# A smaller ring of DMA descriptors and two more slots for expert weights

## The chip, the cores and the metric

The kernel runs on one core of a Trainium2 chip. The core has TensorE (PE, matmuls), VectorE (DVE), ScalarE (ACT), GpSimd (POOL) and SyncE (SP); here SyncE issues nearly all DMAs. The metric is the device time of one execution in microseconds; lower is better.

## The reference

One layer of an encoder block on 256 tokens of width 1024, in float32. A normed input goes through one wide projection; its columns feed sparse attention (16 heads) and a Mamba-2 scan (SSD, 32 heads in 4 groups). Both branches are gated, merged and projected, and the sum goes through a mixture of experts, which is where most bytes are read: all weights of 32 experts, 1024 x 256 for gate and up and 256 x 1024 for down.

```python
h = rmsnorm(x, attn_norm);  proj = h @ w_in
...
x = x + (sigmoid(gate_a) * (y_attn @ w_attn) + sigmoid(gate_b) * (y_ssd @ w_ssd)) @ w_out
hf = rmsnorm(x, ffn_norm)
...
for g in range(4):
    a = einsum('nd,edf->nef', hf, w_gate[g])
    u = einsum('nd,edf->nef', hf, w_up[g])
    act = silu(a) * u * combine[:, g, :, None]
    out = out + einsum('nef,efd->nd', act, w_down[g])
x = x + out
```

`combine` is zero but for two experts of a token.

## The kernel before, in words

**Dense part (to some 385 us).** The weights of the projections come as chunks `w0` to `w37`. Class `Chunk` (line 130) issues their loads on SyncE (`w_raw`, line 141); `split_hi` on ScalarE (line 152) and `split_lo` on VectorE or GpSimd (line 156) cut each into two float32r parts, `w_hl`, which TensorE uses in three passes (lines 241, 294). A `w_raw` load waits until the buffer that it overwrites has been split; four such buffers are cycled.

**Order of the work.** The program is written as Python loops, and a scheduler that simulates a time line sets the order in which each engine issues its instructions. The loop at line 808 takes the SSD groups 1 to 3: for each of four chunks it multiplies, then calls `prefetch(PF0[4 * g + i])`, then one step of the scan of the group before. `PF0` (line 1199) has a string for each of these 12 places and for 4 behind them; a letter is one chunk of expert weights that is loaded there, and names the pool of buffers that it goes to.

**Expert part.** The experts' weights are 96 chunks of 128 partitions x 4 experts x 512 numbers (8 KB of a partition, 1.05 MB): eight quarters `q` (0 to 7) of four experts, each with eight chunks for gate and up (`wgu`, k = 0 to 7) and four for down (`wdn`). `prefetch` (line 255) loads the next chunk on SyncE:

```python
n = len(ewt)
q, i = divmod(n, 12)
src = wgu[q, i] if i < KD else wdn[q, i - KD]
etags.append(tag)
m = 2 if tag in "RSG" else 4
for e in range(0, 4, m):
    w = bigt([P, m, 512], F32, f"we{q}_{i}", tag)
    for cols in (slice(0, 256), slice(256, 512)) if n == 95 else (slice(0, 512),):
        nc.sync.dma_start(w[:, :, cols], src[:, e:e + m, cols])
```

Letters R, S and G take a chunk in two pieces of two experts, so with two loads; the other letters take it whole. The last chunk, 95, is loaded in two halves of its columns besides. The letters of the dense part are the slots of a ring: `ring = list(etags)` (line 1013), and chunk n takes the slot of chunk n less the number of slots, once TensorE has used that one (line 1016). Before the change the ring has 23 slots: five E, two H, two A, four of `PF1`, three of `PFO`, and two R, three S and two G at line 914.

A quarter is: gather of its tokens by matmul (line 1030), gate and up (line 1037), the activation on ScalarE and VectorE (lines 1073 to 1076), transposes (line 1079), down (line 1097), and the sum over experts into `acc` (line 1112). In the last quarter `warm2` (line 862) puts matmuls without use between these steps. The output is copied and stored from line 1114 on. A fallback for overfull experts (line 1124) is not taken.

`kernel` (line 1297) builds the program. The memory that is kept for GpSimd's ring of DMA descriptors has its default size, 16 KB of a partition.

Of the kernel before, what the change touches and what calls it, by code (L numbers as in the profile page):

```python
# [48 lines left out]
def block_kernel(ctx, tc, xin, idn, ngain, catt, cprep, cssd, cmoe, cwr, wsm, wwide, win, wgu, wdn, out, dbg=None):  # L49
# [205 lines left out]
    def prefetch(tags):  # L255

        for tag in tags:
            n = len(ewt)
            if n == 96:
                return  # L260
# [4 lines that stand above are left out]
            v = []  # L265
            with tc.issue_after(last_raw[0].ins):
# [4 lines that stand above are left out]
                    v += [w[:, j, :] for j in range(m)]  # L271
            ewt.append(v)
# [513 lines left out]
    def steps(g, names):  # L786

        for n in names:
            with tc.high_priority(HP["XEYT".index(n.upper())]):
                if n in "Xx":  # L790
                    ssd_x(g, "Xx".index(n))
                elif n in "Ee":
                    ssd_e(g, "Ee".index(n))
                elif n in "Yy":
                    ssd_y(g, "Yy".index(n))
                elif g:
                    ssd_tail(g - 1)
# [10 lines left out]
    for g in range(3):  # L808
        for i, c in enumerate(group_chunks(g + 1)):
            c()  # L810
            prefetch(PF0[4 * g + i])
            steps(g, SEQ[i])
    for c in range(2):
        def half(i):
            prefetch(PF0[12 + i])
            steps(3, SEQ[i])
# [379 lines left out]
XD = 2  # L1196
YB = 2
SEQ = ("XE", "xYTe", "y", "")
PF0 = ('EEEEE',) + 10 * ('',) + ('HH', '', '', '', 'AA')
NE = "".join(PF0).count("E")  # L1200
XB = 3
ZB = 2
# [107 lines left out]
```

## Time and profile before

| | us |
|---|---|
| median of 3 runs | 589.68 (589.41 to 589.89) |
| profiled execution | 591.09 |
| its span, first to last instruction | 589.3 |
| TensorE busy | 558.2 (95%) |
| VectorE, ScalarE, GpSimd busy | 331.0, 272.1, 241.8 |
| bytes moved | 159.27 MB, mean 270 GB/s |

The profile is of one execution whose own time is 1.4 us above the median; 1.8 us of it lie outside the span. Busy time of TensorE is modelled at its ends and includes waits of the pipeline, so a share of 95% isn't a share of its peak. The profile's share of a DMA engine counts the time of its packets, so a mean share of 1.01 means that all 16 are always busy. "Landing" is the time from the issue of a load to its arrival.

### The profile page before, as it was taken

How to read it: one execution, taken by the hardware profiler on the slowest of the kernel's cores; microseconds unless marked ns; L12 is line 12 of the kernel's file. 1: busy time of each engine (PE TensorE's matmuls, PEld its weight loads, DVE VectorE, ACT ScalarE, POOL GpSimd, SP SyncE). 2: the span in 40 equal slices, each digit the busy share in tenths (PEclk: the TensorE clock that was granted, in tenths of full speed). 3: DMA queues.
4: the chain of work that ended last, by engine and by line, in shares of the span. 5: the costliest groups of instructions: out<-in, count | busy, mean ns of one | idle time of the engine just before them, and what ended most of it. 6: DMA issues, size and time to landing. Idle time of an engine off the chain costs nothing.

```text
span 589.3 us, 9910 instructions
## 1 busy us (share of the span) xinstructions
PE 558.2 (95%) x3605; PEld 401.8 (68%) x3605; DVE 331.0 (56%) x689; ACT 272.1 (46%) x633; POOL 241.8 (41%) x254
## 2 busy tenths in 40 slices
PE   8999989999999999999999999999898898896996
PEld 5878768798898999888878888954353354241422
DVE  4669974999995888999595656441111211110101
ACT  7567567658897688877763535500000000000001
POOL 5677685666764376575767644210000000000000
PEclk9999999999999999999999999999999998987899
DMA  6755244353434585445767599999999999999994
GB/s 269 253 176 180 71 160 162 118 182 132 131 122 161 177 365 208 143 137 162 252 220 254 176 329 409 400 340 414 418 413 414 418 419 409 417 419 420 409 412 140
DMA packets 35811, 159.27 MB, mean 270 GB/s; under 512 B 4144, under 2 KB 5808, under 8 KB 27184
## 3 DMA queue, kind: packets, MB, share of 16 engines
q1 hardware_dynamic: 34464, 157.30, 70.8%
q10 hardware_dynamic: 1296, 1.30, 0.6%
q8 instruction: 30, 0.49, 0.3%
q14 instruction: 21, 0.17, 0.1%
HBM read 157.54 MB, written 1.05 MB: 269 GB/s over the span
## 4 chain that ended last, share of the span: by engine, by line
PE 71%; DMA 14%; DVE 7%; issue 3%; POOL 3%; ACT 2%; SPq 0%; ACTq 0%; DVEq 0%; POOLq 0%
DMA we<-wgu 8%; PE ps_xs L241 8%; PE ps_S L294 7%; PE pgu L1037 6%; PE ps_z L241 6%; PE ps_g L294 6%; DMA we<-wdn 5%; PE py L1097 4%; PE ps_g L1030 4%; PE ps_A L294 4%; PE acc L1112 3%; PE ps_q L294 2%; PE ps_o L241 2%; PE ps_o L294 2%; PE ps_iq L294 2%
## 5 line engine op out<-in xcount | busy, mean ns | idle before, releaser
L156 POOL TENSOR_TENSOR w_hl<-w_raw,w_hl 128x512 fp32r<-128x512 f32 (+1 forms) x101 | 140.9, 1399 | 88.2 <-ACT w_hl L152 67.2
L152 ACT CAST w_hl<-w_raw 128x512 fp32r<-128x512 f32 (+1 forms) x212 | 125.7, 619 | 49.1 <-PE ps_S L294 19.0
L156 DVE TENSOR_TENSOR w_hl<-w_raw,w_hl 128x512 fp32r<-128x512 f32 (+1 forms) x111 | 98.5, 895 | 37.3 <-ACT w_hl L152 36.6
L1037 PE MATMUL pgu<-we,xg 128*32 128x512 f32 x512 | 63.1, 603 | 4.0 <-DMA we<-wgu 4.0
L1055 POOL TENSOR_TENSOR dc<-Dm,cmr 128x128 f32<-128x128 f32 x16 | 6.1, 401 | 141.2 <-DVE Dm L960 135.1
L241 PE MATMUL ps_z<-hT,w_hl 128*128 128x256 f32 x384 | 51.5, 286 | 0.0
L241 PE MATMUL ps_xs<-hT,w_hl 128*128 128x256 f32 x384 | 50.7, 285 | 0.0
L241 PEld LDWEIGHTS ps_z<-hT,w_hl 128*128 128x128 f32 x384 | 47.7, 190 | 2.0 <-issue 1.8
L241 PEld LDWEIGHTS ps_xs<-hT,w_hl 128*128 128x128 f32 x384 | 47.5, 191 | 2.1 <-issue 2.1
L294 PE MATMUL ps_g<-w_hl,gT 128*128 128x512 f32 x192 | 47.9, 398 | 0.0
L294 PE MATMUL ps_S<-w_hl,yT 128*128 128x512 f32 x192 | 44.9, 392 | 0.0
L1033 DVE TENSOR_TENSOR xg<-ps_g,cmoe 128x512 f32<-128x512 f32 (+2 forms) x18 | 11.3, 631 | 57.2 <-PE ps_g L1030 57.1
L1030 PEld LDWEIGHTS ps_g<-Dm,x_sb 128*128 128x128 f32 x256 | 31.3, 191 | 17.0 <-issue 13.5
L1037 PEld LDWEIGHTS pgu<-we,xg 128*32 128x32 f32 x512 | 15.3, 110 | 40.0 <-issue 25.9
L1097 PE MATMUL py<-we,aTt 128*32 128x512 f32 (+1 forms) x272 | 37.7, 683 | 3.9 <-DVE aTt L1083 2.1
L294 PEld LDWEIGHTS ps_g<-w_hl,gT 128*128 128x128 f32 x192 | 35.1, 188 | 8.8 <-issue 0.8
L294 PEld LDWEIGHTS ps_S<-w_hl,yT 128*128 128x128 f32 x192 | 35.7, 188 | 7.6 <-issue 0.2
L1075 DVE SCALAR_TENSOR_TENSOR ac<-th,pgu 128x256 f32<-128x256 f32 x8 | 3.4, 421 | 59.9 <-ACT th L1073 59.9
L1108 ACT COPY y<-py 128x512 f32<-128x512 f32 (+1 forms) x9 | 4.8, 538 | 67.2 <-PE py L1097 67.2
L1030 PE MATMUL ps_g<-Dm,x_sb 128*128 128x128 f32 x256 | 33.8, 280 | 0.0
L1112 PE MATMUL acc<-y,dcT 128*128 128x512 f32 (+1 forms) x68 | 32.4, 604 | 0.9 <-DVE y L1110 0.8
L1073 ACT ACTIVATE th<-pgu,rs 128x256 f32<-128x256 f32 x8 | 3.8, 473 | 59.6 <-PE pgu L1037 59.6
(296 smaller groups left out, 976.2 us busy)
## 6 DMA issues: line engine op xcount, KB each, us to landing
we<-wgu SPq DMA_DIRECT2D x42, 1024.0 KB, 14.3
w_raw<-wwide SPq DMA_DIRECT2D x60, 512.0 KB, 3.7
we<-wdn SPq DMA_DIRECT2D x25, 1024.0 KB, 13.9
w_raw<-win SPq DMA_DIRECT2D x44, 512.0 KB, 3.7
we<-wgu SPq DMA_DIRECT2D x44, 512.0 KB, 10.3
we<-wdn SPq DMA_DIRECT2D x14, 512.0 KB, 10.2
x_sb<-xin SPq DMA_DIRECT2D x2, 512.0 KB, 4.3
w_raw<-wsm SPq DMA_DIRECT2D x1, 512.0 KB, 5.5
```

The costliest lines, as they stand in the source:

```text
L152: return act.copy(self.hl[i][:, 0], self.raw[i])
L156: return eng.tensor_sub(hl[:, 1], self.raw[i], hl[:, 0].bitcast(F32))
L241: pe.matmul(ps, lhsT=lhs[k][:, a], rhs=rhs[k][:, b], start=j == 0 and k == 0 and i == 0, stop=j == len(regions) - 1 and k == KD - 1 and i ...
L294: pe.matmul(ps[t], lhsT=lhs[t][k][:, a], rhs=w[k][:, b], start=k == 0 and i == 0, stop=k == KD - 1 and i == 2)
L1030: pe.matmul(ps[:, kk, :], lhsT=x1[:, t, (k + kk) * P:(k + kk + 1) * P], rhs=Dm[:, t].rearrange("p e j -> p (e j)"), start=t == 0, stop=t == 1)
L1033: dve.tensor_tensor(xg[:, ks, :], ps, fgain[:, ks].unsqueeze(2).to_broadcast([P, n, P]), op=ALU.mult)
L1037: i = pe.matmul(pgu[32 * e:32 * e + 32, :], lhsT=xg[:, k, 32 * e:32 * e + 32], rhs=wg[k][e], start=k == 0, stop=k == KD - 1, tile_position ...
L1055: pool.tensor_tensor(dc[:, t], Dm[:, t], cmr[:, t, 4 * q:4 * q + 4].unsqueeze(2).to_broadcast([P, 4, NSLOT]), op=ALU.mult)
L1073: act.activation(th, pgu[:, 0:256], AF.Tanh, scale=rs)
L1097: i_py = pe.matmul(py[32 * e:32 * e + 32, :], lhsT=aTt[:, f, 32 * e:32 * e + 32], rhs=wd[2 * n + f][e][:, c], start=f == 0, stop=f == 1, t ...
L1108: act.copy(y, py)
L1112: pe.matmul(acc[t][n][:, c], lhsT=dcT[:, t * P:(t + 1) * P], rhs=y, start=False, stop=q == 7 and c.stop == 512)
```

## The change

The memory kept for GpSimd's descriptors is set to 512 bytes of a partition. `PF0` has two more letters E, at the places 5 and 7 (group 2's second and fourth chunk of the loop), so `NE`, the number of buffers of pool E, becomes 7, and the ring 25 slots. The chunks that are loaded at the later places are each two further on, and the slots R, S and G now hold other chunks.

```diff
-PF0 = ('EEEEE',) + 10 * ('',) + ('HH', '', '', '', 'AA')
+PF0 = ('EEEEE',) + 4 * ('',) + ('E', '', 'E', '', '', '', 'HH', '', '', '', 'AA')
 NE = "".join(PF0).count("E")
...
-    nc = _bacc.Bacc("TRN2", target_bir_lowering=False, num_devices=1)
+
+    nc = _bacc.Bacc("TRN2", target_bir_lowering=False, num_devices=1, dynamic_dma_scratch_size=512)
```

First, SyncE's queue in the dense part, behind the first five chunks (`we_4` is chunk 4 of a quarter, `w_raw` the weights for the split); the difference:

```order
 L270 DMA we_3_2497<-wgu 128x2048
 L270 DMA we_4_2499<-wgu 128x2048
-L141 DMA w_raw<-win 128x1024 x12
+L141 DMA w_raw<-win 128x1024 x2
+L270 DMA we_5_3004<-wgu 128x2048
+L141 DMA w_raw<-win 128x1024 x4
+L270 DMA we_6_3228<-wgu 128x2048
+L141 DMA w_raw<-win 128x1024 x6
 L141 DMA w_raw<-wwide 128x1024 x5
```

Chunks 5 and 6 are issued among the loads of `w23` to `w28`; where chunk 5 stood, behind `wwide`, there is now chunk 7.

Second, TensorE in the last quarter, the down matmuls of the second half of the columns (`we_10` is chunk 94, `we_11` chunk 95, `acc` the sum over experts, `py` the product for 32 slots of an expert). Before:

```order
L1097 MATMUL py<-we_10_5701,aTt 32x256 x4
L1112 MATMUL acc_4740<-y,dcT 128x512
L1112 MATMUL acc_4742<-y,dcT 128x512
L1097 MATMUL py<-we_10_5701,aTt 32x256 x4
L1097 MATMUL py<-we_11_5703,aTt 32x256 x8
L1112 MATMUL acc_4741<-y,dcT 128x256
```

Now:

```order
L1097 MATMUL py<-we_10_5689,aTt 32x256 x2
L1097 MATMUL py<-we_10_5691,aTt 32x256 x2
L1097 MATMUL py<-we_11_5693,aTt 32x256 x2
L1112 MATMUL acc_4744<-y,dcT 128x512
L1112 MATMUL acc_4746<-y,dcT 128x512
L1097 MATMUL py<-we_10_5689,aTt 32x256 x2
L1097 MATMUL py<-we_10_5691,aTt 32x256 x2
L1097 MATMUL py<-we_11_5693,aTt 32x256 x2
L1097 MATMUL py<-we_11_5696,aTt 32x256 x4
L1112 MATMUL acc_4745<-y,dcT 128x256
```

Both chunks now are in two pieces, and two matmuls on the first piece of chunk 95 stand ahead of the sums of the first half (`acc` 128x512), which stood right behind chunk 94.

Third, SyncE's last loads of quarter 7. Before:

```order
L270 DMA we_6_5689<-wgu 128x1024
L270 DMA we_6_5691<-wgu 128x1024
L270 DMA we_7_5693<-wgu 128x1024
L270 DMA we_7_5695<-wgu 128x1024
L270 DMA we_8_5697<-wdn 128x2048
L270 DMA we_9_5699<-wdn 128x2048
L270 DMA we_10_5701<-wdn 128x2048
L270 DMA we_11_5703<-wdn 128x4x256 x2
```

Now:

```order
L270 DMA we_6_5679<-wgu 128x2048
L270 DMA we_7_5681<-wgu 128x2048
L270 DMA we_8_5683<-wdn 128x2048
L270 DMA we_9_5685<-wdn 128x1024
L270 DMA we_9_5687<-wdn 128x1024
L270 DMA we_10_5689<-wdn 128x1024
L270 DMA we_10_5691<-wdn 128x1024
L270 DMA we_11_5693<-wdn 128x2x256 x2
L270 DMA we_11_5696<-wdn 128x2x256 x2
```

The chunks of gate and up came in halves and are now whole, and the last three down chunks were whole (95 by columns) and now come in pieces.

In the dense part the scheduler also orders TensorE, VectorE, ScalarE and GpSimd differently from the second half of group 1's steps on; the instructions are the same.

## Rows read from the trace of the kernel before

**Rows 1.** The page, busy share of the 16 DMA engines in 40 slices.
```profile
DMA  6755244353434585445767599999999999999994
```
**Rows 2.** Windows of all engines: start:end, length, busy (count), granted clock, DMA share, GB/s.
```profile
40.00:80.00 40.00, 38.23 (x187) 30.34 (x185) 35.50 (x68) 24.20 (x50) 28.87 (x31) 1.00 0.42 140
260.00:280.00 20.00, 20.00 (x153) 16.89 (x152) 20.00 (x40) 15.17 (x33) 11.89 (x10) 1.00 0.49 149
390.00:392.00 2.00, 2.00 (x20) 1.57 (x20) 0.00 (x0) 0.00 (x0) 0.00 (x0) 1.00 0.60 111
400.00:420.00 20.00, 19.44 (x136) 9.81 (x138) 3.81 (x9) 0.99 (x3) 0.76 (x2) 1.00 1.01 422
480.00:500.00 20.00, 17.89 (x131) 7.27 (x131) 3.41 (x9) 1.06 (x3) 0.76 (x2) 0.91 1.01 413
```
**Rows 3.** The chain in order of time, 370 to 590 us: start, length, what.
```profile
437.91 7.05 PE pgu L1037 x64
...
480.13 7.05 PE pgu L1037 x64
...
501.99 11.37 DMA we<-wdn
...
562.36 15.15 DMA we<-wdn
...
578.29 1.91 PE acc L1112 x4
```
**Rows 4.** Timeline of SyncE, 390 to 391 us: start, length, engine, line, operation.
```profile
390.15 0.33 SPq L270 DMA_DIRECT2D we<-wdn  x1
```
**Rows 5.** Line 270, issued 513.2 to 531.3 us (x8: min/median/max ns, first to last).
```profile
L270 SPq EVENT_SEMAPHORE  x8: 17/17/17, 513.4 to 530.8; - x8
...
DMA to landing us min/median/max: 19.9/19.9/19.9
```
**Rows 6.** Line 270, issued 550.6 to 559 us: halves of chunks.
```profile
L270 SPq DMA_DIRECT2D we<-wgu x7: 328/328/328, 550.8 to 558.5; - x7
...
DMA to landing us min/median/max: 10.1/10.2/10.2
```
**Rows 7.** Line 270, issued 563.5 to 566 us: the column halves of chunk 95.
```profile
L270 SPq DMA_DIRECT2D we<-wdn x2: 549/602/655, 563.6 to 564.9; - x2
...
DMA to landing us min/median/max: 15.3/15.4/15.5
```
**Rows 8.** The page, DMA queues: packets, MB, share of 16 engines' time.
```profile
q1 hardware_dynamic: 34464, 157.30, 70.8%
q10 hardware_dynamic: 1296, 1.30, 0.6%
```
**Rows 9.** Line 141, issued 210 to 215 us: loads for the split.
```profile
L141 SPq DMA_DIRECT2D w_raw<-win x2: 327/328/328, 210.8 to 213.6; - x2
...
DMA to landing us min/median/max: 11.9/12.0/12.1
```
**Rows 10.** The page, DMA issues: count, KB each, median us to landing.
```profile
w_raw<-win SPq DMA_DIRECT2D x44, 512.0 KB, 3.7
```
**Rows 11.** Waits of TensorE, 200 to 345 us: total, times, longest. The only row.
```profile
PE py L749 <- DVE e L734: 0.2, 1, 0.2
```
**Rows 12.** Windows of all engines, columns as in rows 2: quarters 6 and 7.
```profile
538.00:539.00 1.00, 0.68 (x4) 0.20 (x8) 0.00 (x0) 0.00 (x0) 0.00 (x0) 0.50 0.99 410
548.00:549.00 1.00, 1.00 (x10) 0.70 (x7) 0.00 (x0) 0.00 (x0) 0.00 (x0) 0.94 0.92 377
562.00:569.00 7.00, 5.89 (x30) 0.87 (x25) 0.00 (x0) 0.00 (x0) 0.00 (x0) 1.00 1.04 420
```
**Rows 13.** Timeline of TensorE, 535 to 570 us, with the idle time before a piece.
```profile
538.32 1.94 PE L1037 MATMUL pgu<-we,xg 128*32 128x512 f32 x8 [1.44 <-DMA we<-wgu]
543.13 5.24 PE L1097 MATMUL py<-we,aTt 128*32 128x512 f32 x24 [0.56 <-issue]
563.62 1.05 PE L1037 MATMUL pgu<-we,xg 128*32 128x512 f32 x4 [0.23 <-DMA we<-wgu]
```

## The prediction

> **What bounds the kernel now.** I read the 40 slices first, then the windows, then the chain in order of time, then the transfers behind the last waits.
>
> The slices show two regimes [rows 1]: in the first 23 of 40 the DMA engines are busy for 2 to 8 tenths, and from the 24th on they are full almost to the end. The windows give them numbers [rows 2]: at 260 to 280 us TensorE is busy for all of its 20.00 us while DMA moves 149 GB/s; at 400 to 500 us DMA has a share of 1.01 at 413 to 422 GB/s.
>
> The chain says what that costs [rows 3]. From 390 to 502 us it runs through TensorE, which has a store of loaded weights: the gate/up work of quarters 2 and 4 begins at 437.91 and 480.13 us, so a quarter takes TensorE 21.1 us when nothing is missing. From 501.99 us it is DMA in unbroken pieces up to the landing at 562.36 + 15.15 = 577.51 us, and 11.8 us of tail follow. A quarter is 12 chunks of 1.05 MB, and a chunk lands every 2.49 us (eight issues from 513.4 to 530.8, each 19.9 us to landing) [rows 5], so DMA needs 29.9 us for what TensorE does in 21.1. The end of the kernel is therefore the end of the loads.
>
> When do the loads begin to count? After the first 23 chunks: at 390.15 us SyncE issues the first load that waited for a used slot [rows 4]. Just then the queue has run dry: 111 GB/s from 390 to 392 us [rows 2]. So the end is the time of this first release, plus (96 less the number of slots) loads, plus the tail. The chunks loaded before it cost nothing as long as DMA has room, and it has.
>
> **The change part by part.** *The descriptor ring.* Loads run in the two hardware queues [rows 8], and no DMA is issued on GpSimd's queue. Making its ring small removes and adds no instruction; it frees 16,384 - 512 = 15,872 bytes of a partition, and two slots of 8,192 bytes need 512 more, which were spare. Cost nothing.
>
> *Two loads come early.* Chunks 5 and 6 are issued behind two, and then four more, of the weight loads that follow the first five chunks (first order piece). They add 2.1 MB to a stretch that moves 149 GB/s [rows 2]. What is queued behind them on SyncE are the loads of weights for the split. Without company such a load lands in 3.7 us [rows 10]; before, two of them were issued right behind five chunks at once and landed in 11.9 to 12.1 us [rows 9]. Yet TensorE waited in the whole of 200 to 345 us only once, 0.2 us, and for VectorE [rows 11]. One chunk in front costs 2.5 us, a third of the 8.3 that were hidden already. I cost it at nothing; with no cover at all it would be 2 x 2.49 = 5.0 us.
>
> *Two loads fewer after the first release.* 71 instead of 73: -2 x 2.49 = -4.98 us. The release itself depends on TensorE, and the last 18 slots are filled at the same places as before; so I leave it, with its dry queue, where it was. The rows leave 2.49 or 2.54 us (1.05 MB at 413 GB/s [rows 2]) for a chunk; I take the landings.
>
> *Halved chunks.* Seven slots of the ring take a chunk as two loads. Such halves land every (558.5 - 550.8)/6 = 1.28 us [rows 6], 2.56 for a chunk, 0.07 more than a whole one. With 23 slots 21 of the chunks after the release are halved, with 25 only 16 (chunk 95, cut in both, aside): -5 x 0.07 = -0.35 us. Together -5.3 us.
>
> *The tail.* Now chunk 95 falls into a slot in two pieces and each is loaded in two column halves: four loads instead of two. TensorE's order changes with it (second order piece): the four matmuls that finish the first half of the output now stand behind two matmuls on chunk 95's first quarter. Before, chunk 94 landed at 577.51 and 95 in halves at 563.6 + 15.3 = 578.9 and 564.9 + 15.5 = 580.4 us [rows 3, 7], while those four matmuls ran from 578.29 us [rows 3]. So half of chunk 95 takes 1.4 us and a quarter 0.7: chunk 94 now at 572.2, the quarter at 572.9, the four matmuls at 573.1, 5.2 us earlier than before. So 0.1 us goes back.
>
> *The clock in quarter 7.* Before, its last gate/up chunks came as halves, with TensorE idle 0.23 us before each [rows 13], and the granted clock was 1.00 (2.4 GHz) from 562 to 569 us [rows 12] and through the tail. Now chunks 84 to 92 are whole. The nearest row is quarter 6, whose chunks came whole: TensorE idle for 1.44 us before its last [rows 13], and the clock fell to 0.50 (1.2 GHz) by 538 us [rows 12]. It rose only at 548 us, when 4.8 us of the steady work from 543.13 on had run at 1.2 GHz [rows 12, 13]. If that repeats, 4.8 us of the steady work (filler included) behind the last gate/up chunk runs at half speed and ends 2.4 us later; the wait for chunk 95's quarter, 0.7 us, hides some of it: 1.7 us. The ends are 0, if the clock holds, and 3.4, if it comes back after twice that work. I take 0.9, half of the price that the nearest row gives, since chunk 95 and the fillers may hide more.
>
> *The new order of the dense part* moves no instruction to another engine; TensorE's wait of 0.2 us there [rows 11] is all that it could win, and what it could lose is a rival below. I take 0.
>
> Sum: -5.3 + 0.1 + 0.9 = **-4.3 us**: the profiled span of 589.3 becomes 585.0, the profiled run 591.09 becomes 586.8. The median of the runs is 589.68, so I predict **585.4 us**. TensorE does not become the bound before that: from 480.13, three more quarters of 21.1 and one to finish end at 564.5 us, ahead of 572.
>
> By the Trainium skill, page DMA: Bandwidth & Descriptors, section Bandwidth (Where 436 GB/s comes from), the HBM side binds a load at about 358 GB/s for a core. By that, two chunks would be an estimated 2.1 MB / 358 GB/s = 5.86 us, and the sum 0.9 us lower. The trace does not agree, with 413 to 422 GB/s [rows 2], and decides.
>
> **The rivals.**
>
> *Late weights (0.11).* The split loads behind chunks 5 and 6 come too late, TensorE stands, and the release slides by the same amount. For it: VectorE is busy for 20.00 of 20 us at 260 to 280 us [rows 2], so lost time there is not made up. Against it: five chunks in front cost nothing [rows 9, 11]. It gives back up to 5.0 (590.4 us), with half of that exposed 587.9 us. The Trainium skill, page DMA: Bandwidth & Descriptors, section Queues, rings and completion order, says that each DMA engine takes the descriptors of a ring in their order, which speaks against a chunk ahead of a needed load. The trace agrees on the delay (12 us against 3.7), but not that it reaches TensorE.
>
> *The clock stays low into the tail (0.08).* As above with 3.4 instead of 0.9: 587.9 us. For it: quarter 6 needed ten microseconds from fall to rise [rows 12]. Against it: the filler matmuls keep TensorE at work there.
>
> *The new order starves TensorE (0.04), the slower side.* The scheduler moves splits, exponentials and conv steps against each other on VectorE, ScalarE and GpSimd from the second group on. The nearest row of such a stretch that is fed badly is 40 to 80 us: TensorE 38.23 of 40.00 busy, VectorE 35.50 [rows 2], a loss of 0.044 us for each us. Over the 143 us from 207 to 350 that is 6.3 us, and the release slides by as much: 589.68 - 4.3 + 6.3 = 591.7 us. It decides from 4.3 us on, and is seen as slower from 5.5. Against it: in that stretch TensorE waited 0.2 us [rows 11].
>
> *More than two chunks (0.03).* The last loads came slower than the rest: 95's end at 580.4 is 11.8 us behind 568.6, where four chunks at 2.49 would take 10.0 [rows 6, 7]. If smaller last loads remove this and the clock holds, 582.7 us.
>
> *The ring does not grow (0).* The order shows 25 chunks ahead of the first load of a used slot, so this is out.
>
> **How the numbers follow.** The forecast, with a tail cost of 0 to 2.4, has 0.74 and reaches from 584.4 to 586.9. The range is **583.6 to 588.0**: up, it takes in the tail cost of 3.4 and half of the late weights; down, a tail cost of 0 and 0.8 us from the last loads. A measurement of this kernel tells 0.2% (1.2 us) from no change. Faster (under 588.5): 0.74 + 0.03 + 0.06 of the low clock + 0.06 of the late weights = 0.89; same 0.02 + 0.05 = 0.07, the rest of these two; slower 0.04.
>
> **What would show it.** Right: the first load of a used slot near 390 us, 25 chunks before it; loads at about 2.5 us each; the last one landing near 575 us; no wait of TensorE for split weights before 350 us. The clock between 550 and 575 us says which tail cost it was. Wrong: a release later than 391 us, DMA below full share between 393 and 572 us, or a last landing that is less than 4 us earlier.

## The result, and the profile after

The changed kernel takes 584.59 us (median, 584.32 to 585.10), the kernel before beside it 589.54: a ratio of 0.9899, 95% interval 0.9884 to 0.9915, or 4.95 us less. A second comparison gave 0.9907 (0.9892 to 0.9923). The forecast was 585.4 us with a range of 583.6 to 588.0: the direction is right, the time is held by the range, and the gain is 0.7 us larger than forecast. Two of its terms, however, were off by as much or more, in opposite directions.

The profiled execution took 585.1 us with a span of 583.3, which is 6.0 us less than the span before. On the page, first the busy times, then the granted clock and the share of DMA in 40 slices, then loads by size (count, KB each, median us to landing):

```profile
PE 552.6 (95%) x3605; PEld 400.6 (69%) x3605; DVE 330.9 (57%) x689; ACT 271.8 (47%) x633; POOL 239.5 (41%) x254
...
PEclk9999999999999999999999999999989997999989
DMA  7755244453435488645568589989999999999993
...
we<-wgu SPq DMA_DIRECT2D x55, 1024.0 KB, 13.8
...
we<-wgu SPq DMA_DIRECT2D x18, 512.0 KB, 10.2
```

The two regimes of [rows 1] are still there. DMA is full from the 25th slice on, one 8 in the 27th aside; before, it was from the 24th. The clock's last 8 stands in the 39th slice (554 to 569 us), which is quarter 7; there it was 1.00 before [rows 12]. The windows show the fall itself (columns as in [rows 2]):

```profile
390.00:392.00 2.00, 2.00 (x17) 1.04 (x16) 0.00 (x0) 0.00 (x0) 0.00 (x0) 1.00 0.78 209
400.00:420.00 20.00, 19.44 (x138) 9.72 (x140) 3.15 (x8) 0.96 (x2) 0.76 (x2) 1.00 1.01 420
480.00:500.00 20.00, 17.09 (x116) 6.49 (x105) 2.65 (x5) 0.47 (x1) 0.38 (x2) 0.83 1.01 419
...
562.00:564.00 2.00, 2.00 (x9) 0.13 (x2) 0.00 (x0) 0.20 (x1) 0.00 (x0) 0.50 1.01 399
565.00:566.00 1.00, 1.00 (x7) 0.63 (x6) 0.28 (x2) 0.00 (x0) 0.00 (x0) 1.00 1.02 410
```

The chain in order of time answers to [rows 3]:

```profile
437.15 7.05 PE pgu L1037 x64
...
479.04 7.05 PE pgu L1037 x64
...
498.98 11.39 DMA we<-wdn
...
541.82 19.88 DMA we<-wgu
561.74 1.94 PE pgu L1037 x8
...
572.51 1.91 PE acc L1112 x4
```

Before, DMA held the chain until 577.51 us; now it holds it only until 541.82 + 19.88 = 561.70, and from there on TensorE does, to the end. The gate/up piece at 561.74 takes 1.94 us instead of 1.06, as the one ahead of it: it runs at a granted clock of 0.50, which is 1.2 GHz. The timeline of TensorE shows what it did before (idle time and its cause in brackets), and answers to [rows 13]:

```profile
559.25 1.06 PE L1037 MATMUL pgu<-we,xg 128*32 128x512 f32 x8 [1.44 <-DMA we<-wgu]
561.74 1.94 PE L1037 MATMUL pgu<-we,xg 128*32 128x512 f32 x8 [1.43 <-DMA we<-wgu]
563.61 2.03 PE L867 MATMUL ps_w<-on 128*128 128x512 bf16 x6
```

SyncE's timeline has the first load of a used slot, for [rows 4], and line 270 the last load of all (issued at 565.0):

```profile
389.39 0.33 SPq L270 DMA_DIRECT2D we<-wgu  x1
...
L270 SPq DMA_DIRECT2D we<-wdn x1: 368/368/368, 565.0 to 565.0; - x1
...
DMA to landing us min/median/max: 8.0/8.0/8.0
```

So the last bytes land at 573.0 us; before it was 580.4 [rows 7]. TensorE's waits from 200 to 345 us are again one row, of 0.2 us, as in [rows 11], though at another place:

```profile
PE ps_A L294 <- DVE acc L603: 0.2, 1, 0.2
```

The span divides at three points: the first expert load (206.64 us before, 207.35 after), the first gate/up matmul (389.02 and 388.26 in TensorE's timeline), and the last landing (580.4 and 573.0).

| stretch, us | before | after | difference |
|---|---|---|---|
| start to first expert load | 206.64 | 207.35 | +0.7 |
| to the first gate/up matmul | 182.38 | 180.91 | -1.5 |
| to the last landing | 191.4 | 184.7 | -6.7 |
| to the end of the span | 8.9 | 10.3 | +1.4 |

From the first gate/up matmul to the first load of a used slot it is 1.13 us in both. The prediction had 0 for the second line, -5.3 for the third, +1.0 for the fourth. The first line, and a part of the third, vary from one execution of a kernel to the next, as the traces of the experiments show; those ask where the rest of each line comes from.

### The profile page after: what moved, and what is told of

The parts are those of the page before. It is cut to its first block, busy times and chain, and to the rows that moved or that the text cites. A ratio compares the mean times of both kernels' runs of the same rounds, so it can differ in the third digit from the quotient of the medians.

```text
span 583.3 us, 9898 instructions
## 1 busy us (share of the span) xinstructions
PE 552.6 (95%) x3605; PEld 400.6 (69%) x3605; DVE 330.9 (57%) x689; ACT 271.8 (47%) x633; POOL 239.5 (41%) x254
## 3 DMA queue, kind: packets, MB, share of 16 engines
HBM read 157.54 MB, written 1.05 MB: 272 GB/s over the span
## 4 chain that ended last, share of the span: by engine, by line
PE 69%; DMA 12%; DVE 9%; issue 4%; POOL 3%; ACT 3%; SPq 0%; ACTq 0%; POOLq 0%; DVEq 0%
PE ps_S L294 8%; PE pgu L1037 6%; PE ps_xs L241 6%; PE ps_g L294 6%; DMA we<-wdn 5%; DMA we<-wgu 5%; PE ps_z L241 5%; PE py L1097 4%; PE ps_A L294 4%; PE acc L1112 4%; PE ps_g L1030 4%; PE ps_q L294 3%; PE ps_o L241 2%; PE ps_o L294 2%; PE ps_iq L294 2%
## 5 line engine op out<-in xcount | busy, mean ns | idle before, releaser
L156 DVE TENSOR_TENSOR w_hl<-w_raw,w_hl 128x512 fp32r<-128x512 f32 (+1 forms) x111 | 100.4, 911 | 38.7 <-ACT w_hl L152 38.1
L1037 PE MATMUL pgu<-we,xg 128*32 128x512 f32 x512 | 60.2, 603 | 3.9 <-DMA we<-wgu 3.9
L1097 PE MATMUL py<-we,aTt 128*32 128x512 f32 (+1 forms) x272 | 35.8, 616 | 3.8 <-DVE aTt L1083 2.1
## 6 DMA issues: line engine op xcount, KB each, us to landing
we<-wdn SPq DMA_DIRECT2D x17, 1024.0 KB, 17.4
```

The source lines that it names most:

```text
L156: return eng.tensor_sub(hl[:, 1], self.raw[i], hl[:, 0].bitcast(F32))
L1037: i = pe.matmul(pgu[32 * e:32 * e + 32, :], lhsT=xg[:, k, 32 * e:32 * e + 32], rhs=wg[k][e], start=k == 0, stop=k == KD - 1, tile_position ...
L1097: i_py = pe.matmul(py[32 * e:32 * e + 32, :], lhsT=aTt[:, f, 32 * e:32 * e + 32], rhs=wd[2 * n + f][e][:, c], start=f == 0, stop=f == 1, t ...
```

## Experiments

Each kernel was timed four to twelve times beside the kernel before, whose medians in these comparisons were 589.8 to 590.5 us; ratios are to it, with 95% intervals. Each is told with its edit, to the kernel before where the letters or the memory of the old ring are seen in the diff, and to the changed kernel otherwise, unless the text says more.

### Is the small descriptor memory worth anything by itself?

**Only the memory.** 23 slots, and nothing put into the 16 KB:

```diff
-    nc = _bacc.Bacc("TRN2", target_bir_lowering=False, num_devices=1)
+    nc = _bacc.Bacc("TRN2", target_bir_lowering=False, num_devices=1, dynamic_dma_scratch_size=512)
```

> The kernel before with GpSimd's descriptor memory at 512 bytes and still 23 slots. Theory (only the number of slots counts: the end is the first release of a used slot, plus the loads that are left, plus the tail): 589.5 us, within 0.8 of the kernel before, with 73 loads after the release, the last landing 10 us or less before the end of the span as before. Rival (the freed memory or the new order of the dense part is worth something by itself): the release of the first used slot comes 0.7 us earlier than 390.15, and the time is 588.7 or less.

Measured: 595.78 us, 1.0107 (1.0090 to 1.0125). That is 6 us slower, and neither theory had it. The trace tells why. In SyncE's timeline the five first expert chunks go out at 185 us instead of 206.64:

```profile
185.30 3.50 SPq L270 DMA_DIRECT2D we<-wgu  x5
189.58 0.33 SPq L141 DMA_DIRECT2D w_raw<-win  x1
```

The constants `cprep` are loaded at that moment from ScalarE's queue. The view of that tile (its load, who waited for it and for how long, the time to landing):

```profile
L86 ACTq DMA_DIRECT2D cprep<-cprep x1: 339/339/339, 185.4 to 185.4; - x1
...
  ACT prep L651: 2.8, 1
...
DMA to landing us min/median/max: 8.4/8.4/8.4
```

In the kernel before the same load, issued at 186.1 us, landed in 3.9 us (the same view):

```profile
L86 ACTq DMA_DIRECT2D cprep<-cprep x1: 334/334/334, 186.1 to 186.1; - x1
...
DMA to landing us min/median/max: 3.9/3.9/3.9
```

What it holds up is `prep`, and with it TensorE. TensorE's waits from 190 to 200 us, and behind them the windows with the clock:

```profile
PE ps_c L655 <- DVE prep L652: 2.4, 1, 2.4
```
```profile
194.00:197.00 3.00, 1.12 (x10) 1.15 (x11) 2.73 (x10) 2.05 (x5) 1.31 (x1) 1.00 1.01 423
197.00:199.00 2.00, 2.00 (x14) 2.00 (x13) 1.94 (x5) 1.70 (x6) 0.25 (x1) 0.60 1.03 430
199.00:201.00 2.00, 2.00 (x12) 2.00 (x12) 1.92 (x5) 0.89 (x3) 1.04 (x1) 0.55 0.99 414
```

DMA is full with the chunks, TensorE has 1.12 us of work in 3, and then runs at little more than half clock for four. The first gate/up matmul comes at 393.87 instead of 389.02 us, 4.9 us later. The Trainium skill, page DMA: Bandwidth & Descriptors, section Issuing engines are not separate DMA queues, says that DMAs started by different engines run on the same 16 DMA engines and interleave; this trace agrees, with 8.4 us against 3.9 for a small load from another queue.

Why did the chunks go out early? In the kernel before SyncE waits 2.9 us at the first of them for VectorE's `cb` (line 676): by this wait, the E buffers lie over memory that the dense part still uses. With 16 KB free SyncE has no such wait there, so that they seem to lie elsewhere. Two more runs had free memory, one of 8 KB with a slot more, one with a slot fewer:

```diff
-PF0 = ('EEEEE',) + 10 * ('',) + ('HH', '', '', '', 'AA')
+PF0 = ('EEEEE',) + 4 * ('',) + ('E', '', '', '', '', '', 'HH', '', '', '', 'AA')
...
-    nc = _bacc.Bacc("TRN2", target_bir_lowering=False, num_devices=1)
+    nc = _bacc.Bacc("TRN2", target_bir_lowering=False, num_devices=1, dynamic_dma_scratch_size=512)
```

> The small descriptor memory with one letter E more (24 slots, 72 loads after the release). Theory (2.49 us for each slot): 589.54 - 2.49 = 587.0 us, plus or minus 0.8 for the tail, since the last gate/up chunks of quarter 7 fall into other slots: chunks 89 to 91 come in halves here and whole in the changed kernel, so that the granted clock should stay at 1.00 from 555 to 570 us. Rival (two slots are needed for a step in the order of the loads, or the gain comes from which chunks are halved): 589 or more, or 585 or less.

Measured: 593.24 us, 1.0054 (1.0035 to 1.0073), with the same wait of 2.4 us.

```diff
-PF0 = ('EEEEE',) + 10 * ('',) + ('HH', '', '', '', 'AA')
+PF0 = ('EEEE',) + 10 * ('',) + ('HH', '', '', '', 'AA')
```

> The kernel before, default descriptor memory, with one letter E fewer (22 slots, 74 loads after the release). Theory: 589.54 + 2.49 = 592.0 us, plus or minus 0.8 for the tail. Rival (the first release only slides, because the queue is dry at 390 us anyway, or a shorter stretch of loads in the dense part frees TensorE): 590.5 or less.

Measured: 596.99 us, 1.0125 (1.0104 to 1.0146), with a wait of 2.5 us. Both expectations missed, and neither time says anything yet about the number of slots.

**The memory filled.** The first run again, with a buffer that nothing uses where the 16 KB were:

```diff
-    xe = ctx.enter_context(tc.tile_pool(name="xe", bufs=NE, side="right", reuse_waits="tile"))
+    hole = ctx.enter_context(tc.tile_pool(name="hole", bufs=1, side="right", reuse_waits="tile")); hole.tile([P, 2 * 2048], F32, name="hole"); xe = ctx.enter_context(tc.tile_pool(name="xe", bufs=NE, side="right", reuse_waits="tile"))
...
-    nc = _bacc.Bacc("TRN2", target_bir_lowering=False, num_devices=1)
+    nc = _bacc.Bacc("TRN2", target_bir_lowering=False, num_devices=1, dynamic_dma_scratch_size=512)
```

> 23 slots and the small descriptor memory as in the first run, but the 16 KB that are freed are taken by a buffer that nothing uses, next to the pool of the E slots, so that the E buffers lie over the same earlier buffers as before; the order of the instructions is that of the kernel before. Theory (the 6 us of the first run came from free memory: the first five chunks no longer waited for memory that other work still held, went out at 185 us instead of 207, ahead of five loads for the split, and TensorE waited 2.4 us for prep): 589.7 us, within 0.8 of the kernel before, first chunk near 207 us, no wait of ps_c for prep. Rival (a small descriptor memory itself makes DMA or GpSimd slower): 595 us, with the first chunk near 207 all the same.

Measured: 590.01 us, 0.9999 (0.9989 to 1.0009); first chunk at 207.12 us, no wait for `prep`. So the descriptor memory costs and gives nothing by itself. Left free, it costs 6 us; filled with two slots, it pays.

**24 and 22 slots with full memory.** 24 with a descriptor memory that leaves room for one slot only; 22 with the slot's place taken by a buffer:

```diff
-PF0 = ('EEEEE',) + 10 * ('',) + ('HH', '', '', '', 'AA')
+PF0 = ('EEEEE',) + 4 * ('',) + ('E', '', '', '', '', '', 'HH', '', '', '', 'AA')
...
-    nc = _bacc.Bacc("TRN2", target_bir_lowering=False, num_devices=1)
+    nc = _bacc.Bacc("TRN2", target_bir_lowering=False, num_devices=1, dynamic_dma_scratch_size=8192)
```

> 24 slots with a descriptor memory of 8 KB, so that the one further slot takes all that is freed; the first five chunks again stand behind the loads that they stood behind before. Theory (2.49 us for each slot once the dense part keeps its order): 587.2 us, plus or minus 0.8, release of the first used slot between 388.3 and 390.2 us. Rival (the run with 24 slots was slower for a reason that lies in the number, the order of the slots in the last quarter for one): 591 us or more.

Measured: 586.72 us, 0.9937 (0.9923 to 0.9951).

```diff
-    xe = ctx.enter_context(tc.tile_pool(name="xe", bufs=NE, side="right", reuse_waits="tile"))
+    hole = ctx.enter_context(tc.tile_pool(name="hole", bufs=1, side="right", reuse_waits="tile")); hole.tile([P, 1 * 2048], F32, name="hole"); xe = ctx.enter_context(tc.tile_pool(name="xe", bufs=NE, side="right", reuse_waits="tile"))
...
-PF0 = ('EEEEE',) + 10 * ('',) + ('HH', '', '', '', 'AA')
+PF0 = ('EEEE',) + 10 * ('',) + ('HH', '', '', '', 'AA')
```

> 22 slots, default descriptor memory, and the 8 KB of the slot left out are taken by a buffer that nothing uses, so that the first chunks go out near 207 us again. Theory (2.5 us for each slot): one load more after the release than the kernel before, 590.0 + 2.5 = 592.5 us, plus or minus 1.3 for the order of the dense part, which the scheduler changes here too. Rival (the first run with 22 slots was slow because of its number): 596 us or more.

Measured: 593.42 us, 1.0055 (1.0041 to 1.0069). With the memory full, 22, 23, 24 and 25 slots stand at +3.2, 0, -3.7 and -5.5 to -6.0 us (ratios times 590). The slot law holds in sign and about in size; its steps also hold what the dense part and the tail do. By the loads alone it holds closely. From the landing of the fifth load of a used slot to the last landing it is 175.3 us in both traces with 22 slots, 172.8 to 172.9 in the four with 23, 170.3 in both with 24, and 167.3 to 167.8 in the nine with 25, whether the memory was full or not. For the kernel before and the changed one, line 270 from 396.6 to 397.5 and from 395.9 to 396.9 us has that fifth load:

```profile
L270 SPq DMA_DIRECT2D we<-wgu x1: 332/332/332, 396.9 to 396.9; - x1
...
DMA to landing us min/median/max: 10.6/10.6/10.6
```
```profile
L270 SPq DMA_DIRECT2D we<-wgu x1: 332/332/332, 396.2 to 396.2; - x1
...
DMA to landing us min/median/max: 9.3/9.3/9.3
```

By these rows the last landings, at 580.4 and 573.0 us, are 172.9 and 167.5 us behind it. What varies is the time ahead of this landing, in which the queue fills again: from the release to it, it is 17.4 us before the change, and 16.1 and 17.2 us in two executions of the changed kernel.

### Does it matter where the two loads stand?

**Late**, behind the two H at place 11, and **first**, right behind the five:

```diff
-PF0 = ('EEEEE',) + 4 * ('',) + ('E', '', 'E', '', '', '', 'HH', '', '', '', 'AA')
+PF0 = ('EEEEE',) + 10 * ('',) + ('HHEE', '', '', '', 'AA')
```

> 25 slots, small descriptor memory, but the two extra chunks are loaded late in the dense part, behind the two H at place 11, so that the loads for the split up to group 3 have no chunk in front of them. Theory (where the two early loads stand costs nothing): within 0.8 us of the changed kernel's 584.6, and TensorE waits for no split weights between 200 and 345 us in either. Rival (their place decides when the first used slot is released): the release moves away from the changed kernel's 389.39 us by 0.7 us or more, and the time with it.

Measured: 585.15 us, 0.9930 (0.9913 to 0.9947): 4.1 us under the kernel before, 1.4 to 1.8 behind the changed kernel's two comparisons (0.0023 and 0.0031 times 590). By size this is outside the expected 0.8, though the intervals overlap. The dense part tells more than the times do. From the first expert load to the start of `ps_A`, in the timelines of SyncE and TensorE:

```profile
206.04 2.88 SPq L270 DMA_DIRECT2D we<-wgu  x5
...
278.53 2.91 PE L294 MATMUL ps_A<-w_hl,aT 128*128 128x512 f32 x12
```

That is 72.5 us here, as in the kernel before (206.64 to 279.14) and with the memory filled (207.12 to 279.62). In the changed kernel it is 71.2 (207.35 to 278.59, and 205.78 to 277.04 in the second comparison), and with 24 slots too (207.49 to 278.75). So where the loads stand at places 5 and 7, or one at 5, the stretch is 1.3 us shorter, without any wait less. The lines of TensorE from 150 to 390 us show how (busy us, mean ns of one). Before:

```profile
L749 PE MATMUL py<-e,xdt 128*64 128x256 f32 x64 | 11.7, 404 | 0.2 <-DVE e L734 0.2
...
L716 PE MATMUL ps_x<-ident,xs 128*128 128x128 f32 x32 | 6.2, 279 | 0.0
```

After:

```profile
L749 PE MATMUL py<-e,xdt 128*64 128x256 f32 x64 | 11.3, 404 | 0.0
...
L716 PE MATMUL ps_x<-ident,xs 128*128 128x128 f32 x32 | 5.3, 274 | 0.0
```

The 32 and 64 matmuls of these two lines cover 0.9 and 0.4 us less of TensorE's time: each is as long as before to 2%, but in the new order more of them overlap. The whole stretch says the same. Its windows, with columns as in [rows 2], are those of the kernel before, the loads late, 24 slots with full memory, and the changed kernel:

```profile
206.64:279.14 72.50, 72.29 (x587) 65.22 (x586) 67.92 (x116) 57.47 (x128) 47.50 (x39) 1.00 0.58 204
206.04:278.53 72.49, 72.29 (x587) 65.23 (x586) 67.92 (x116) 57.49 (x128) 47.54 (x39) 1.00 0.60 227
207.49:278.75 71.26, 71.08 (x589) 65.06 (x588) 66.34 (x111) 56.60 (x127) 45.80 (x39) 1.00 0.61 230
207.35:278.59 71.24, 71.08 (x590) 65.04 (x588) 66.35 (x111) 56.56 (x127) 46.07 (x39) 1.00 0.68 244
```

TensorE's matmuls of the dense part stand in one order in the first two and in another in the last two. The late version has two expert loads more in this stretch than the kernel before, issued at 269.78 and 270.25 us, and the changed kernel has one more than 24 slots; neither moves the stretch by more than 0.02 us. So it is the order that is worth 1.3 us here and not the loads beside it. All twelve traces with one of the two orders agree: 72.5 us in four, 71.2 or 71.3 in eight. Which overlap in the pipeline makes the difference no run shows.

```diff
-PF0 = ('EEEEE',) + 4 * ('',) + ('E', '', 'E', '', '', '', 'HH', '', '', '', 'AA')
+PF0 = ('EEEEEEE',) + 10 * ('',) + ('HH', '', '', '', 'AA')
```

> 25 slots and the small memory, with the two extra chunks at the first place, so that seven chunks in a row stand ahead of the loads for groups 1 to 3, from about 207 us on. Theory (a chunk in front of these loads costs nothing after 207 us, since there is cover): 584.9 us, plus or minus 0.8, the loads for the split behind the seven land in 16 to 18 us, and TensorE waits for none of them. Rival (late weights: the cover of the five chunks is used up): a wait of TensorE for split weights or what is made of them between 210 and 260 us, the release at 391 us or later, 587 us or more.

Measured: 586.75 us, 0.9945 (0.9927 to 0.9962), some 2.5 us slower than with the loads at places 5 and 7. The rival holds in its mechanism, and its 587 us are missed by 0.25. TensorE's waits from 200 to 392 us, and line 141 from 209 to 216 us:

```profile
PE ps_S L294 <- DVE w_hl L156: 1.8, 1, 1.8
PE ps_z L241 <- DVE w_hl L156: 1.6, 1, 1.6
PE py L749 <- DVE yg L755: 0.8, 1, 0.8
PE ps_lg L911 <- ACT xT L907: 0.2, 1, 0.2
```
```profile
L141 SPq DMA_DIRECT2D w_raw<-win x2: 327/328/328, 209.9 to 212.8; - x2
...
DMA to landing us min/median/max: 17.3/17.9/18.4
```

Behind seven chunks the split loads land in 17.9 us instead of 12.0 [rows 9], and the wait for `ps_z` follows at 240.9 us. (The profiled execution was 3.3 us above the median of this kernel, so these rows show the place of the loss, not its size.) "Late weights" is a real price, which the places 5 and 7 avoid.

### The tail: clock, filler, last loads

**Gate/up chunks 88 to 91 in halves**, into the same slots:

```diff
-                        nc.sync.dma_start(w[:, :, cols], src[:, e:e + m, cols])
+                        h = 2 if 88 <= n < 92 else m
+                        for j in range(0, m, h):
+                            nc.sync.dma_start(w[:, j:j + h, cols], src[:, e + j:e + j + h, cols])
```

> The changed kernel with the last four gate/up chunks of quarter 7 loaded in two pieces of two experts each, into the same slots. Theory (the clock fell at 561.5 us because TensorE stood for 1.4 us ahead of each whole chunk, and the filler and the down matmuls behind it ran late for it): idle time of about 0.2 us per piece, granted clock 1.00 from 555 us on, the sums of the first half (acc 128x512) 1.2 us earlier than 572.5, and 583.4 us. Rival (the last landings set the tail, and the clock only fills the wait for them): sums not more than 0.4 us earlier, 584.3 us or more.

Measured: 583.97 us, 0.9889 (0.9873 to 0.9905). The clock is 1.00 from 556 us on, idle time ahead of a half 0.23 us, and the sums start at 571.48 us, 183.1 us behind the first gate/up matmul instead of 184.2 in the changed kernel. The mechanism is as expected; the time lies between the two theories, and is not told apart from the changed kernel's.

**The changed kernel again**, beside the next three:

> The changed kernel unaltered, beside the next three on the same chip. Every theory: ratio to the kernel before 0.990 plus or minus 0.002, some 5.9 us of 590; gate/up work begins near 388.4 us, the clock falls to 0.50 for about 3 us near 562.

Measured: 584.81 us, 0.9907 (0.9892 to 0.9923). Here the clock fell at 558.5 us and was back only after 565: the view of windows has

```profile
561.00:565.00 4.00, 4.00 (x14) 0.96 (x15) 0.85 (x2) 0.47 (x1) 0.00 (x0) 0.50 1.01 404
```

so the fall lasts about 3 us in one execution and 7 in another.

**Four filler matmuls behind each of the gate/up chunks 5 and 6**, chunks whole:

```diff
-WT = (0, 0, 6, 4, 8, 4)
+WT = (4, 4, 6, 4, 8, 4)
```

> The changed kernel, whole chunks, with four filler matmuls behind each of the gate/up chunks 5 and 6 of quarter 7, so that TensorE's idle time ahead of the last two chunks shrinks from 1.44 to some 0.4 us. Theory (the clock falls because of that idle time, and costs about 1 us): clock 1.00 from 556 us on, sums of the first half about 1 us earlier than in the changed kernel, and as fast as the version with halved gate/up chunks, 0.6 us under the changed kernel. Rival (the fall comes from something else in quarter 7, or the loads set the tail): clock 0.50 near 562 again, or the same time as the changed kernel within 0.3 us.

Measured: 583.12 us, 0.9882 (0.9866 to 0.9899), 1.7 us under the changed kernel beside it. In TensorE's timeline:

```profile
558.70 1.06 PE L1037 MATMUL pgu<-we,xg 128*32 128x512 f32 x8 [0.46 <-DMA we<-wgu]
559.70 1.04 PE L867 MATMUL ps_w<-on 128*128 128x512 bf16 x4
561.20 1.06 PE L1037 MATMUL pgu<-we,xg 128*32 128x512 f32 x8 [0.47 <-DMA we<-wgu]
...
570.48 1.98 PE L1112 MATMUL acc<-y,dcT 128*128 128x512 f32 x4
```

Idle time has gone from 1.43 to 0.47 us, the piece takes 1.06 instead of 1.94, and from the last landing (564.7 + 7.9 = 572.6) to the end of the span of 581.3 it is 8.7 us, as before the change (8.9). So the fourth line of the table was the clock.

**The same filler in the kernel before**, whose last gate/up chunks come in halves (the edit is the same line, made to the kernel before):

```diff
-WT = (0, 0, 6, 4, 8, 4)
+WT = (4, 4, 6, 4, 8, 4)
```

> The kernel before with the same four filler matmuls behind gate/up chunks 5 and 6 of quarter 7. Its chunks come in halves and its clock is 1.00 there, so there is nothing to win. Theory (the filler pays only through the clock): the kernel before plus or minus 0.4 us, or up to 1 us slower where filler stands in front of a half that has landed. Rival (filler there helps by itself): 1 us or more faster than the kernel before.

Measured: 591.39 us, 1.0020 (1.0008 to 1.0032), 1.2 us slower. So filler does not help by itself. It pays where it keeps the clock and otherwise stands in the way.

**Fewer loads at the end.** In the changed kernel SyncE's last load waited 2.9 us, by its waits for a `wdn` load: the last quarter of chunk 95 goes out at 565.0, when the load eight before it (chunk 92) has landed. With halved gate/up chunks, and chunk 95 in two loads:

```diff
-                    for cols in (slice(0, 256), slice(256, 512)) if n == 95 else (slice(0, 512),):
+                    for cols in (slice(0, 256), slice(256, 512)) if False else (slice(0, 512),):
```

> Halved gate/up chunks as in the run before, and chunk 95 in two loads instead of four (no column halves). In the changed kernel the last load went out only at 565.0 us, since SyncE waits before each load until the one eight loads earlier has landed, here chunk 92. With two loads the last one waits for the first half of chunk 91 and goes out near 561. Theory (this wait leaves DMA partly empty from 567 us on, and so sets the last landing): DMA keeps 400 GB/s to 570 us, last landing 571.5 or earlier instead of 573.0 to 573.8, and 1 us or more under the version with halved gate/up chunks alone. Rival (the engines run out unevenly anyway, or the last matmuls then wait for all columns): the same time within 0.4 us, or slower.

Measured: 584.79 us, 0.9894 (0.9875 to 0.9912). And with three:

```diff
-                    for cols in (slice(0, 256), slice(256, 512)) if n == 95 else (slice(0, 512),):
+                    for cols in (slice(0, 256), slice(256, 512)) if n == 95 and e else (slice(0, 512),):
```

> As the run before, but the second piece of chunk 95 still in two column halves: three loads, the last one waits for the second half of chunk 91 and goes out near 562. Theory: like the run before or up to 0.4 us faster, since the last load is half as large. Rival: as there.

Measured: 583.55 us, 0.9883 (0.9868 to 0.9898). The last loads go out at 561.4 and 560.7 us, and the last landings are 573.0 and 572.2 us, 185.4 and 184.8 behind the first gate/up matmul, against 184.7 and 185.8 in the two executions of the changed kernel. The rival holds: an earlier last issue moves no landing. That this is because DMA runs out unevenly anyway is argued, not shown.

**Filler and three loads together**, whole gate/up chunks:

```diff
-                    for cols in (slice(0, 256), slice(256, 512)) if n == 95 else (slice(0, 512),):
+                    for cols in (slice(0, 256), slice(256, 512)) if n == 95 and e else (slice(0, 512),):
...
-WT = (0, 0, 6, 4, 8, 4)
+WT = (4, 4, 6, 4, 8, 4)
```

> The changed kernel with the four filler matmuls behind gate/up chunks 5 and 6 of quarter 7, and chunk 95 in three loads (its first piece whole). Theory (both last waits gone: the clock holds, and the last load goes out near 561 us instead of 564.7): ratio to the kernel before 0.987, up to 0.6 us under the version with filler alone. Rival (the last landing is set by how DMA runs out, not by the wait): the same as with filler alone within 0.4 us.

Measured: 582.80 us, 0.9873 (0.9855 to 0.9892). It is the fastest median of all, but can't be told apart from the filler alone, and it wasn't run beside the changed kernel. Filler alone was, and beats both kernels: its four runs (582.75 to 584.33) lie under the four of the changed kernel (584.54 to 585.01).

## Why the prediction was right or wrong

Two steps of the sum failed. The new order of the dense part was put at 0 and was worth -1.3 us, and the clock in quarter 7 was put at +0.9 and cost 1.4 to 1.7. The loads, the largest term, came out as forecast.

**What bounds the kernel: right.** The end is the first release, the loads left, and the tail. The first load of a used slot came at 389.39 us, 25 chunks were ahead of it, DMA was full from 393 to 567 us, and the last landing was 7.4 us earlier, where "wrong" was set at less than 4. One sign of being wrong was set too sharply: DMA "below full share" ahead of 572 us. Its share was 0.82 at 569 to 571 us, 2 to 4 us ahead of the last landing, as it was 0.91 at 575 to 577 us before, 3 to 5 us ahead.

**The descriptor ring at nothing: right, but the reason was not the whole of it.** It was argued from the ring alone, and with the memory filled the ratio is 0.9999. But the memory has a second use: when it is free, the first loads lose the wait that kept them behind the load of `cprep`, and 6 us are lost. The change is free of that only because its second part fills the memory to the brim. The two parts were costed one by one, and they are not independent.

**Two loads early at nothing: right for these places.** No wait of TensorE for split weights was seen from 200 to 388 us. The rival "late weights" had the right mechanism, and with the loads at the first place it costs 2.5 us of the 5.0 that the prediction bounded it by.

**Two loads fewer, -4.98, and the halved chunks, -0.35: right.** From first release to last landing it was 190.2 us (390.15 to 580.4) and is 183.6, which is -6.6 and looks like more than the 5.3. But the second execution of the changed kernel has 184.7 (387.62 to 572.3), and the run with the memory filled has 189.6 (390.43 to 580.1), so that such pairs give anything from -5.0 to -6.6. From the fifth landing on, behind the refilling of the dry queue, it is 172.8 us before and 167.6 and 167.5 in the two executions of the changed kernel: -5.3, as forecast. How much of it the halved chunks are was not measured apart. For the rival "more than two chunks" nothing is left, and the two runs on the last loads moved no landing either.

**The dense part's new order at 0: wrong.** "TensorE's wait of 0.2 us there [rows 11] is all that it could win" is the sentence that failed. The stretch to `ps_A` became 1.3 us shorter with no wait less. A busy share of 20.00 of 20 us does not say that the same work can't be done in less: the old order was busy for 72.29 us there and the new one for 71.08, where the matmuls of the two lines shown above were as long as before to 2%.

**The clock in quarter 7, +0.9: right in kind, mis-sized.** The clock fell to 0.50 exactly where the chunks came whole with 1.43 us of idle time. The filler run prices it at 1.7 us, the tails of the profiled executions at 1.4 (8.9 and 10.3 us). The 1.7 is what the prediction had worked out from quarter 6 and then halved, since chunk 95 and the fillers might hide more; they hid little or nothing of it. That the figures agree so well is partly luck, as the low clock lasted 3 us in one execution and 7 in another. The tail's other 0.1 us wasn't tested apart.

Taken together: -1.3 for the dense part, -5.3 for the loads and +1.4 to 1.7 for the clock make -4.9 to -5.2, where the times show -4.95 and -5.5. What is left is within what one execution differs from the next: the stretch up to the first expert load was 206.64 us before, 207.35 after and 205.78 in the second comparison. The two failed terms have opposite signs, so that the forecast came within 0.8 us of the time is in part luck.

## What to carry to other kernels

Memory that is freed and not used is not neutral where buffers lie over one another: it removes waits that kept transfers apart, so measure the freeing with the space filled, and then with the new use. Where loads bound the end, price a slot by the landings, look for what a whole chunk in the place of two halves does to TensorE's idle time and clock, and put filler into just those gaps. In a stretch where TensorE is always busy, still allow for one or two per cent when a scheduler reorders it (1.3 of 72.5 us here). And before a term is called mis-sized from one pair of traces, look at a second trace of the same kernel: here the time from the first release to the last landing differed by 1.0 us between two executions of one kernel, all of it ahead of the fifth landing.

## What was not expected of the hardware

- A load of constants from ScalarE's queue took 8.4 us instead of 3.9 when five chunks of 1.05 MB went out on SyncE's queue from 185.3 us on, 0.1 us ahead of it.
- With idle times of 1.03, 1.44 and 1.43 us, one after the other between pieces of work of 1.06 us, the granted clock fell to 0.50; with idle times of 0.23 us it did not. For two long ones alone the traces show both: with 1.28 and 1.43 us (22 slots, memory full) and 1.22 and 1.42 us (ahead of the filler) the clock stayed at 1.00, and in quarter 6 of the kernel before, with 1.42 and 1.44 us, it fell to 0.50. The low clock lasted 3 us in one execution of the changed kernel and 7 in another.
- The same matmuls in another order took 1.3 us less in a stretch where TensorE waited for 0.2 us in either order, and this repeated to 0.03 us within each order (twelve traces).
- From the fifth load of a used slot on, the loads of different executions of kernels with 23 slots took the same time to within 0.1 us (172.8 to 172.9), while the time from the release to that landing varied from 16.5 to 17.4 us.
